# Strassen once more inside one product: S3 T3 of the second input phase as seven inner products

## The chip, the cores and the metric

The kernel runs on one core of one Trainium2 chip. The metric is the device time of that core in microseconds. TensorE multiplies; it reads both operands from the on-chip memory (SBUF) and adds into accumulators (PSUM, here eight banks of 128 x 512 float32). VectorE and ScalarE do elementwise work and can read and write PSUM. SP, ScalarE and GpSimd (POOL) issue transfers between chip memory and HBM. Every engine takes its instructions in program order and waits on semaphores.

## The reference

One layer is computed: an RMS norm, an input projection 1024 -> 2048, a causal pooling mixer, a gate, an output projection, a residual and a final norm. x has 4096 rows of 1024.

```python
normed = rms_norm(h, norm_w)
u, gate = split(normed @ in_w, 2)                       # 1024 -> 1024 + 1024
pooled = stack([trailing_mean(u_g, w) for w in (2, 4, 8, 16)]) - u   # 4 groups of 256 channels
mixed = einsum('bsgc,gcd->bsgd', pooled, group_w) + group_b
y = mixed * scale * silu(gate)
h = h + y @ out_w
out = rms_norm(h, final_norm_w)
```

Everything is float32. The kernel gets that precision from TensorE by splitting each operand into a high part (a copy rounded to the faster fp32r format) and a low part (the difference), and adding three products: high x high, high x low, low x high.

## The kernel before, in words

**Tiles.** The rows are worked in four blocks of 1024. The group map is folded into the first half of the input projection at the start, so that the kernel has two input products of 1024 x 1024 x 1024 a block (phase a and phase b, each giving 512 of u and 512 of the gate) and the output product (phase o, in eight blocks of 512 rows).

**Strassen.** Each of these products is done as seven products of half size (Winograd's form): of quarters of x and of the weights sums and differences are formed, and the seven results are added up in PSUM or on eviction. The seven are called P1 to P7; P7 is S3 T3, the product of x11 - x21 with w22 - w12. `steps` (line 960) lists them: phase a for four blocks, phase b for four blocks (order P1, P2, P6, P7, P5, P4, P3, line 32), phase o for eight. A step of phase a or b is 8 units (two halves h of the contraction by four column tiles ct), a unit is 6 matmuls of width 512 into one bank (`product_in`, 587; `mm3`, 576): 48 matmuls. A step of phase o has 24.

**Banks.** P1, P2, P7 and P4 go to banks 0 to 3, P6, P5 and P3 to banks 4 to 7 (line 585). ScalarE evicts or copies on (`evict_in`, 710), VectorE adds.

**Order of the work around a step.** The main loop (line 1204) gives, at step n: the loads for step n + 3, the sums for n + 2 (`form_in`), the split of the operands of n + 1 (`split_in`, `split_halves`: ScalarE writes the high part, VectorE the low one, into one of four operand tiles in turn, `next_op`), pooling work that is due (`pool`, about 10 us of VectorE), then the matmuls and the eviction of step n. A scheduler places the instructions of each engine by its own priorities; `tc.issue_after` holds one behind another, `tc.high_priority` moves it ahead.

**Tiles to work in.** Eleven `st` and eight `vt` tiles of 128 x 1024 are handed out by `take` and given back by `give`; a load into a tile waits until the last reader is done, and SP, which issues nearly all loads and stores, waits with it.

**Weights.** `w[i]` holds the split weights of product i, two tiles of 1 MB. Those of phase b are formed during block 3 of phase a and block 0 of phase b (`load_wb`, `form_wb`, `split_wb`), from parts in HBM: `wvd`, the folded map, and `t3d`, its difference t3, which `save_t3` (274, called at P6 of block 2, line 1249) loads, subtracts and stores. Those of phase o are formed in blocks 1 and 2 of phase b (`make_wo`, 320), stored in `wod`, and loaded and split by `load_w` (328) in block 3, each behind the step whose place it takes.

**Pooling.** `pool` (628) evaluates the trailing means, for two groups as a scan on VectorE that ScalarE starts with a short accumulated sum (`before`, 642).

Of the kernel before, what the change touches and what calls it, by code (L numbers as in the profile page):

```python
# [10 lines left out]
F32 = mybir.dt.float32  # L11
# [50 lines left out]
def kernel(  # L62
# [48 lines left out]
    ops = [mem.tile([P, 4 * H], F32R, tag=f"op{i}", name=f"op{i}") for i in range(4)]  # L111
# [42 lines left out]
    def split(dst, src):  # L154

        latest_split[1] = copy(dst[:, 0], src).ins
        latest_split[0] = sub(dst[:, 1], src, dst[:, 0].bitcast(F32)).ins
# [10 lines left out]
    wvd = [dram.tile([P, 2, H], F32, name=f"wvd{k}") for k in range(4)]  # L168
    t3d = [dram.tile([P, 2, H], F32, name=f"t3d{h}") for h in range(2)]
# [15 lines left out]
    nc.vector.memset(eps, EPS)  # L185
    scrap = const.tile([P, 1], F32, name="scrap")
# [75 lines left out]
    def load_wb(i):  # L262
        for h in range(2):
# [5 lines left out]
            for name, place, used in (("t3", t3d[h], (P6, P7)), ("22", wvd[2 + h], (P5, P3))):  # L269
                if i in used:  # L270
                    p[name] = take()
                    nc.sync.dma_start(out=p[name], in_=place)

    def save_t3():

        for h in range(2):
            us = []
            for k in (h, 2 + h):
                us.append(take())
                nc.sync.dma_start(out=us[-1], in_=wvd[k])  # L280
            with tc.issue_after(evicted[0]):
                sub(us[0], us[1], us[0])
            nc.sync.dma_start(out=t3d[h], in_=us[0])
            for u in us:
                give(u)
# [34 lines left out]
    def make_wo(h):  # L320
        us = {}
        for n in range(2):
            for kh in range(2):
                us[kh, n] = load_rows(out_w, 4 * kh + 2 * h, n * H)
                scale_rows(us[kh, n], pair(scale_c, h, kh))
        store_weights(wod, h, us[0, 0], us[1, 0], us[0, 1], us[1, 1])

    def load_w(src, i):
        for h in range(2):
            u = take()  # L330
            nc.sync.dma_start(out=u, in_=src[i][h])
            split(w[i][h], u)
# [128 lines left out]
    turn = [0]  # L461

    def next_op(pattern, **sizes):
        t = ops[turn[0] % 4]
        turn[0] += 1
        return t.rearrange(pattern, **sizes)
# [3 lines left out]
    def split_halves(us, saved=None, by_pool=False):  # L470
        ts = []
        for h, u in enumerate(us):
            t = next_op("p (s a b) -> p s a b", s=2, a=2)
# [66 lines left out]
    def split_in(q, b, i):  # L540
        s = xs[b]
        key = {P1: "11", P2: "12", P6: "2", P7: "21", P5: "11", P4: "22", P3: "12"}[i]
        later = q == 0 and b == 0 and i in (P1, P2)
# [42 lines left out]

    def product_in(i, t, sets, by_bank, between=None, behind=None):
        ps = sets[bank_of[i]]
# [3 lines left out]
        for n, (h, ct) in enumerate(halves):  # L592
            if between and n in between:
                between[n]()
            c = slice(ct * P, (ct + 1) * P)
            with tc.issue_after(behind) if behind and n == 1 else nullcontext():
                for kk in range(2):
                    mm3(
                        ps[ct],
                        (w[i][h][:, 0, kk, c], w[i][h][:, 1, kk, c]),  # L600
                        (t[h][:, 0, kk], t[h][:, 1, kk]),
                        i in (P1, P7) and h == 0 and kk == 0,
                        h == 1 and kk == 1,
                    )
        if between and 8 in between:
            between[8]()

    def product_out(i, t, sets, last):
        ps = sets[bank_of[i]]
        for j in range(2):  # L610
            rows = slice(j * P, (j + 1) * P)
            size = H // 4 if last and j == 1 else H // 2
            for c in range(0, H // 2, size):
                dst = sets["spare"] if c else ps[j]
                for k in range(4):
# [3 lines left out]
                        (t[:, 0, k, rows], t[:, 1, k, rows]),  # L619
# [8 lines left out]
    def pool(b, q, half, vs, sgs):  # L628
# [3 lines left out]
        end = HIST + H  # L632
        for g in range(2):
# [5 lines left out]
            if run_on and not first:  # L639
                for j in range(2):  # L640
                    junk = small.tile([P, HIST], F32, tag="junk", name=f"junk{b}_{half}_{grp}_{j}")
                    before = small.tile([P, 1], F32, tag="before", name=f"bf{b}_{half}_{grp}_{j}")
# [133 lines left out]
    def split_o(b, i):  # L776
        s = oxs[b]
        t = next_op("p (s a b) -> p s a b", s=2, a=4)
# [215 lines left out]
    def run(n, between=None, behind=None):  # L994
        kind, b, i = steps[n]
        sets = sets_of(kind, b)
        if kind == "o":
            product_out(i, split_up.pop(n), sets, n == len(steps) - 1)
            evict_o(b, i, sets)
        else:  # L1000
# [203 lines left out]
    for n in range(2, len(steps)):  # L1204
# [41 lines left out]
        if 0 <= since < len(ORDER_IN):  # L1246
            form_wb(ORDER_IN[since])
        run(n)
        if kind == "a" and b == 2 and i == P6:
            save_t3()  # L1250
# [71 lines left out]
```

## Time and profile before

| | us |
|---|---|
| median of 3 runs | 917.21 |
| lowest, highest | 916.2, 919.74 |
| the profiled execution's own time | 917.32 |
| its span in the profile | 915.6 |
| TensorE busy | 904.4 (99%) |
| VectorE busy | 703.5 (77%) |
| ScalarE busy | 457.5 (50%) |
| GpSimd busy | 52.6 (6%) |

In the profile's lines the engines are PE (TensorE's matmuls), PEld (its weight loads), DVE (VectorE), ACT (ScalarE), POOL (GpSimd) and SP; a q behind the name is the engine's sequencer, which issues transfers and waits. L581 is line 581. A tile is written as out<-in, without its number. A timeline line has start, length, engine, line, operation, tiles, shapes and how many in a row; in square brackets stands the idle time before it and who ended it. A line of the groups has count | busy time, mean ns of one | idle time of the engine before them. A line of the transfers ends with KB each and the median time from issue to landing. Matmuls are pipelined: one lasts 379 ns in the profile where the next starts much earlier, so the pace is read from starts.

### The profile page before, as it was taken

The page shows a single profiled execution, that of the slowest core. Times are in us where ns is not written, and L with a number is a line of the kernel's source. Part 1 is how long each engine was busy: PE and PEld are TensorE (multiplying, and loading weights), DVE is VectorE, ACT ScalarE, POOL GpSimd, SP SyncE. Part 2 cuts the span into 40 slices and gives each one's busy share as a digit, 9 for nine tenths or more (in the row PEclk, how much of TensorE's full clock was granted, in tenths as well). Part 3 has the DMA queues.
Part 4 walks back from the last instruction along what each step waited for, and adds up shares of the span by engine and source line. Part 5 has one row for each costly group of instructions (what it writes and reads, how often), then busy time and mean ns, then how long its engine had stood idle before and what let it go on. Part 6 is the DMA issues. An engine that isn't in the chain of part 4 may idle for free.

```text
span 915.6 us, 11210 instructions
## 1 busy us (share of the span) xinstructions
PE 904.4 (99%) x4212; PEld 789.0 (86%) x4212; DVE 703.5 (77%) x769; ACT 457.5 (50%) x741; POOL 52.6 (6%) x130
## 2 busy tenths in 40 slices
PE   9999999999999999999999999999999999999996
PEld 7788888888888888888888888888888888888886
DVE  3898994894699997586696589589978677676675
ACT  7869447447345565246345546654423424324333
POOL 0023201001100000000000000000101101001010
PEclk9999999999999999999999999999999999999999
DMA  9986865666756635016614725745746536356122
GB/s 340 401 320 195 316 236 166 214 230 197 264 198 241 250 146 200 24 47 238 244 47 160 257 87 194 246 161 184 252 165 227 163 135 230 128 194 216 37 92 93
DMA packets 66518, 177.02 MB, mean 193 GB/s; under 512 B 6048, under 2 KB 23840, under 8 KB 66464
## 3 DMA queue, kind: packets, MB, share of 16 engines
q1 hardware_dynamic: 59888, 154.78, 47.9%
q10 hardware_dynamic: 4176, 13.65, 3.8%
q0 software_dynamic: 2400, 7.88, 2.5%
q8 instruction: 33, 0.54, 0.2%
q14 instruction: 21, 0.17, 0.1%
HBM read 115.45 MB, written 60.83 MB: 193 GB/s over the span
## 4 chain that ended last, share of the span: by engine, by line
PE 88%; DMA 5%; DVE 3%; ACT 2%; issue 1%; SPq 0%; DVEq 0%; ACTq 0%
PE bank L581 88%; DMA early<-in_wut 2%; DMA st<-in_x 1%; DMA st<-wvd 1%; DMA st<-in_xt 1%; DVE op L146 1%; DMA t3d<-st 1%; PE bank L374 0%; DVE st L146 0%; DVE st L149 0%; ACT early L408 0%; ACT op L152 0%; DVE st L143 0%; DVE vt L143 0%; DVE vt L146 0%
## 5 line engine op out<-in xcount | busy, mean ns | idle before, releaser
L581 PE MATMUL bank<-op,w 128*128 128x512 f32 x2688 | 581.8, 379 | 2.3 <-DVE op L146 1.5
L581 PEld LDWEIGHTS bank<-op,w 128*128 128x128 f32 x2688 | 507.6, 189 | 75.7 <-DVE op L146 2.3
L581 PE MATMUL bank<-w,op 128*128 128x512 f32 (+1 forms) x1356 | 290.3, 377 | 0.0
L581 PEld LDWEIGHTS bank<-w,op 128*128 128x128 f32 x1356 | 254.6, 189 | 35.8
L146 DVE TENSOR_TENSOR op<-st,op 128x1024 fp32r<-128x1024 f32 x127 | 154.6, 1221 | 75.6 <-ACT op L152 75.5
L152 ACT ACTIVATE op<-st 128x1024 fp32r<-128x1024 f32 x127 | 133.1, 1052 | 143.8 <-PE bank L581 128.5
L152 ACT ACTIVATE vt<-bank 128x512 f32<-128x512 f32 x100 | 56.8, 593 | 49.3 <-PE bank L581 42.4
L152 ACT ACTIVATE op<-vt 128x1024 fp32r<-128x1024 f32 x39 | 40.9, 1055 | 78.8 <-PE bank L581 65.7
L924 DVE TENSOR_TENSOR st<-bank,st 128x512 f32<-128x512 f32 x60 | 41.1, 687 | 29.8 <-PE bank L581 29.4
L146 DVE TENSOR_TENSOR st<-st,st 128x1024 f32<-128x1024 f32 x35 | 42.5, 1221 | 19.3 <-DMA st<-sd 8.6
L146 DVE TENSOR_TENSOR op<-vt,op 128x1024 fp32r<-128x1024 f32 x39 | 47.5, 1222 | 9.5 <-ACT op L152 9.5
L194 POOL TENSOR_SCALAR oms<-oss 128x2 f32<-128x2 f32 x14 | 9.2, 658 | 600.0 <-ACT st L813 593.9
L152 ACT ACTIVATE bank<-bank 128x512 f32<-128x512 f32 x48 | 27.8, 580 | 30.7 <-PE bank L581 27.1
L146 DVE TENSOR_TENSOR w<-st,w 128x1024 fp32r<-128x1024 f32 x21 | 25.5, 1221 | 12.4 <-ACT w L152 12.3
L662 DVE TENSOR_TENSOR_SCAN vt<-vt,bf 128x512 f32<-128x512 f32 x28 | 34.5, 1269 | 0.2 <-ACT vt L152 0.2
L143 DVE TENSOR_TENSOR vt<-bank,vt 128x512 f32<-128x512 f32 (+1 forms) x51 | 33.2, 678 | 1.6 <-PE bank L581 1.6
L924 DVE TENSOR_TENSOR vt<-bank,vt 128x512 f32<-128x512 f32 (+1 forms) x37 | 24.8, 673 | 12.0 <-PE bank L581 11.7
L152 ACT ACTIVATE w<-st 128x1024 fp32r<-128x1024 f32 x21 | 21.9, 1053 | 17.9 <-PE bank L581 14.9
L149 DVE TENSOR_TENSOR st<-st,vt 128x1024 f32<-128x1024 f32 x23 | 27.2, 1219 | 3.1 <-DMA st<-in_xt 3.1
L684 DVE SCALAR_TENSOR_TENSOR vt<-vt,vt 128x1024 f32<-128x1024 f32 x24 | 29.1, 1214 | 0.0
L152 ACT ACTIVATE st<-bank 128x512 f32<-128x512 f32 x30 | 17.5, 595 | 22.7 <-PE bank L581 10.8
L817 DVE SCALAR_TENSOR_TENSOR st<-st,ors,st 128x1024 f32<-128x1024 f32 x17 | 21.4, 1281 | 6.1 <-POOL ors L212 6.1
(130 smaller groups left out, 556.0 us busy)
## 6 DMA issues: line engine op xcount, KB each, us to landing
st<-in_x SPq DMA_DIRECT2D x36, 512.0 KB, 5.0
st<-in_xt SPq DMA_DIRECT2D x29, 512.0 KB, 6.6
st<-sd SPq DMA_DIRECT2D x29, 512.0 KB, 5.0
sd<-st ACTq DMA_DIRECT2D x23, 512.0 KB, 3.7
vt<-in_x SPq DMA_DIRECT2D x21, 512.0 KB, 5.1
st<-yd SPq DMA_DIRECT2D x19, 512.0 KB, 4.3
yd<-vt SPq DMA_DIRECT2D x18, 512.0 KB, 2.8
out<-st SPq DMA_DIRECT2D x17, 512.0 KB, 3.6
```

What stands on the lines that cost most here:

```text
L143: nc.vector.tensor_tensor(out=dst, in0=a, in1=b, op=ALU.add)
L146: return nc.vector.tensor_tensor(out=dst, in0=a, in1=b, op=ALU.subtract)
L149: nc.vector.tensor_tensor(out=dst, in0=a, in1=b, op=ALU.mult)
L152: return nc.scalar.activation(dst, src, func)
L194: nc.gpsimd.tensor_scalar(out=ms, in0=ss, scalar1=1.0 / D, scalar2=EPS, op0=ALU.mult, op1=ALU.add)
L581: latest[0] = nc.tensor.matmul(ps, a, b, start=start and n == 0, stop=stop and n == 2, skip_group_check=True).ins
L662: nc.vector.tensor_tensor_scan(s[:, j, at:end], v[:, j, at:end], v[:, j, at - win : end - win], sums_of[j] if sums_of else 0.0, ALU.add, A ...
L684: nc.vector.scalar_tensor_tensor(out=s[:, :, at : at + H], in0=s[:, :, at : at + H], scalar=1.0 / win, in1=v[:, :, HIST:], op0=ALU.mult, o ...
L817: nc.vector.scalar_tensor_tensor(out=us[j], in0=us[j], scalar=rs[:, j : j + 1], in1=fw[0], op0=ALU.mult, op1=ALU.mult,)
L924: partial["added"] = nc.vector.tensor_tensor(out=dst, in0=src, in1=dst, op=ALU.add).ins
```

## The change

Step P7 of phase b is no longer a step of 48 matmuls of width 512. In each of the four blocks it is done as seven inner products, Winograd's form again, on quarters of S3 and T3, each of 12 matmuls of width 256.

- The operands: quarters and four sums of quarters, each split into a high and a low part of half width (`split_inner`). The operand tiles are now eight half-size ones, handed out and given back, one for the high and one for the low part.
- The results: four quarters of banks 0 to 3 (v11, v12, v21, v22). ScalarE clears v11; a quarter that enters a second result is carried on by a ScalarE copy from one PSUM quarter to the next before the following inner product adds to it: after the first, second and fourth inner product. A last difference is taken by VectorE.
- Between the inner products stand the four units of the second half of P6, the step before; P6 and P7 are evicted after that.
- The weights of the seven inner products are formed in block 1 of phase a (`form_wi`) from t3, which is now loaded, formed and saved in blocks 0 and 1, and are stored in HBM (`wid`). Four stay in the place of P7's weights during phase b. Three take the place of P3's weights and are loaded again in each block by GpSimd's queue, as P3's own weights are (`w3d`, saved in block 0).
- Loads of the output projection's weights move ahead of their use by a step (`load_wo`, `load_w` and `split_w`); the short sums for the scans share one tile of four columns a call.

```diff
-    ops = [mem.tile([P, 4 * H], F32R, tag=f"op{i}", name=f"op{i}") for i in range(4)]
+    ops = Slots([mem.tile([P, 2 * H], F32R, tag=f"op{i}", name=f"op{i}") for i in range(8)])
...
     def split_in(q, b, i):
         s = xs[b]
+        if q and i in INNER:
+            inner.update(us=s[key], sums={}, ops={})
+            with tc.high_priority():
+                split_inner(M_ORDER[:4])
+            return None
...
+    INNER = (P7,)
+    M_ORDER = (P1, P6, P2, P7, P3, P5, P4)
...
+    def split_inner(ms):
+        us, sums_in, ts = inner["us"], inner["sums"], inner["ops"]
+        q = {(h, th): quarter(us, h, th) for h in range(2) for th in range(2)}
+        for m in ms:
+            if m == P6:
+                tiles = inner["tiles"] = [
+                    take("p (m a b) -> p m a b", m=2, a=2) for _ in range(2)
+                ]
...
+                add(sums_in[P5], q[0, 1], q[1, 1])
+                sub(sums_in[P6], sums_in[P5], q[0, 0])
+            elif m == P7:
...
+                sub(sums_in[P7], q[0, 0], q[0, 1])
+            elif m == P3:
...
+                sub(sums_in[P3], q[1, 0], sums_in[P6])
...
+            ts[m] = ops.take(lambda t: t.rearrange("p (s a b) -> p s a b", s=2, a=2))
+            split((by_side(ts[m][:, 0]), by_side(ts[m][:, 1])), src)
...
+    def mm_inner(m, banks_of, j, th):
+        t, wm = inner["ops"].pop(m), wi[M_ORDER.index(m)]
+        for c in range(2):
+            ps = banks_of[2 * j + c][:, th * 256 : (th + 1) * 256].rearrange(
+                "p (a s) -> p a s", s=2
+            )
+            cols_of = slice(c * P, (c + 1) * P)
+            for kk in range(2):
+                for n, (sw, sr) in enumerate(((0, 0), (0, 1), (1, 0))):
+                    latest[0] = nc.tensor.matmul(
+                        ps, wm[:, sw, kk, cols_of],
+                        t[:, sr, kk].rearrange("p (s a) -> p a s", s=2),
+                        start=False,
...
+    def inner_product(i, sets, fill):
...
+        def carry(dst, src):
+            with tc.high_priority():
+                for c in range(2):
+                    inner["copied"] = copy(dst[c], src[c]).ins
+
+        mm_inner(P1, ps, 0, 0)
+        with tc.high_priority():
+            split_inner([P4])
+        carry(v12, v11)
+        fill.pop(0)()
+        fill.pop(0)()
+        mm_inner(P6, ps, 1, 0)
+        carry(v21, v12)
+        fill.pop(0)()
+        mm_inner(P2, ps, 0, 0)
+        mm_inner(P7, ps, 0, 1)
+        u3 = inner["tiles"][0][:, 0]
+        carry(v22, v21)
+        carry([u3[:, 0], u3[:, 1]], v21)
+        fill.pop(0)()
+        mm_inner(P3, ps, 1, 0)
+        mm_inner(P5, ps, 1, 1)
+        for c in range(2):
+            sub(u3[:, c], v22[c], u3[:, c])
+        for c in range(2):
+            add(v12[c], v12[c], u3[:, c])
+        give(inner["tiles"][0])
+        mm_inner(P4, ps, 0, 1)
...
+    def load_wi(ms):
+        for m in ms:
+            nc.gpsimd.dma_start(out=wi[m], in_=wid[m].bitcast(F32R))
...
+    def load_w3():
+        for h in range(2):
+            nc.gpsimd.dma_start(out=w[P3][h], in_=w3d[h].bitcast(F32R))
...
+    def store_wi(src):
+        behind, after = latest_split[0], evicted[0]
+        for m, b in src.items():
+            u = take("p (s a b) -> p s a b", s=2, a=2)
+            r = u.bitcast(F32R)
+            with tc.issue_after(behind):
+                with tc.issue_after(after):
+                    copy(r[:, 0], b)
+                sub(r[:, 1], b, u[:, 0])
+            nc.sync.dma_start(out=wid[M_ORDER.index(m)], in_=u)
+            give(u)
...
+        elif is_inner(n):
+            evict_in(b, 1, i, sets)
+        elif is_inner(n + 1):
+            t = split_up.pop(n)
+            clear_inner(steps[n + 1][2], sets)
+            for ct in range(4):
+                unit(i, t, sets, 0, ct)
+            give_ops(t[0])
+            with tc.high_priority():
+                split_inner(M_ORDER[4:6])
+            inner_product(
+                steps[n + 1][2], sets, [lambda ct=ct: unit(i, t, sets, 1, ct) for ct in range(4)]
+            )
...
-        if kind == "a" and b == 2 and i == P6:
-            save_t3()
...
+        if kind == "a" and b == 0 and i == P4:
+            load_t3(0)
+        elif kind == "a" and b == 0 and i == P3:
+            save_t3(0)
+            load_t3(1)
+        elif kind == "a" and b == 1 and i == P1:
+            save_t3(1)
+        if kind == "a" and b == 1:
+            k = ORDER_LATER.index(i) - 1
+            if 0 <= k < 5:
+                form_wi(k)
+        if since == 2:
+            new_wi()
+            load_wi(range(4))
...
+        if i == P3 and kind == "b" and b + 1 < NB or kind == "a" and b == NB - 1 and i == P3:
+            load_wi(range(4, 7))
+        if kind == "b" and b == 0 and i == P6:
+            load_wb(P3)
+        elif kind == "b" and b == 0 and i == P7:
+            with tc.issue_after(evicted[0]):
+                split_wb(P3)
+            save_w3()
+        elif kind == "b" and i == P7:
+            load_w3()
...
             if kind == "b" and b == NB - 1:
-                load_w(wod, i)
+                if i == P1:
+                    load_w(wod, i)
+                split_w(i)
+                if i != P3:
+                    load_w(wod, ORDER_IN[ORDER_IN.index(i) + 1])
```

194 lines of the change are left out of this document (152 added, 42 removed).

## The prediction

> **What bounds the kernel now.** I read the page's totals first, then TensorE's timeline and waits, then the other engines around the steps that the change touches.
>
> ```profile
> span 915.6 us, 11210 instructions
> PE 904.4 (99%) x4212; PEld 789.0 (86%) x4212; DVE 703.5 (77%) x769; ACT 457.5 (50%) x741; POOL 52.6 (6%) x130
> PEclk9999999999999999999999999999999999999999
> PE 88%; DMA 5%; DVE 3%; ACT 2%; issue 1%; SPq 0%; DVEq 0%; ACTq 0%
> ```
>
> TensorE is busy 99% of the span at full clock and carries 88% of the chain that ended last. Only TensorE's work, or a new wait of TensorE, can move the time. Its timeline gives the price of a product (start, us, instruction, count, idle before it):
>
> ```profile
> 0.78 3.57 PE L1026 MATMUL bank<-const-bfloat16-1.0 128*128 128x512 bf16 x8 [0.78 <-PEq L1307]
> 11.57 5.55 PE L374 MATMUL bank<-w,w 128*128 128x256 f32 x43
> ...
> 249.81 5.99 PE L581 MATMUL bank<-op,w 128*128 128x512 f32 x27
> 256.76 23.44 PE L581 MATMUL bank<-op,w 128*128 128x512 f32 x106 [0.96 <-DVE op L146]
> ...
> 861.71 10.52 PE L581 MATMUL bank<-w,op 128*128 128x512 f32 x48
> 905.74 2.84 PE L581 MATMUL bank<-w,op 128*128 128x256 f32 x24
> ```
> ```profile
> L581 PE MATMUL bank<-w,op 128*128 128x512 f32 x1332 | 287.7, 379 | 0.0
> L374 PE MATMUL bank<-w,w 128*128 128x256 f32 x48 | 6.2, 288 | 0.0
> L581 PE MATMUL bank<-w,op 128*128 128x256 f32 x24 | 2.8, 275 | 0.0
> ```
>
> The last instruction of a run overlaps nothing, so the pace is (length - one duration) / (count - 1): wide (512) (10.52 - 0.38)/47 = 215.8 ns; narrow (256) in the last products (2.84 - 0.28)/23 = 111.5 ns; narrow in the fold (5.55 - 0.29)/42 = 125 ns. One input product of 48 wide matmuls is 10.36 us. From 60 us to the end TensorE waits once:
>
> ```profile
> PE bank L581 <- DVE op L146: 1.0, 1, 1.0
> ```
>
> That is the 0.96 us at 256.76, in P1 of block 3. Unstalled, the 28th matmul after 249.81 would start at 255.64; it is 1.12 late, and the following 106 run at (23.44 - 0.38)/105 = 219.6 ns, 0.40 us above pace (a second late operand). Together 1.52 us.
>
> **The change part by part.**
>
> *Seven inner products.* Per block 48 x 215.8 = 10.36 us go and 7 x 12 = 84 narrow ones come. Bounds: 84 x 111.5 = 9.37 (-0.99) and 84 x 125 = 10.5 (+0.14). I take 111.5: those rows come from the same kind of call, with a moving operand woven from two sides like the new one; the fold reads it in one run. Four blocks: **-3.97 us** (between -3.97 and +0.6). The Trainium skill (TensorE: Matmul & The Clock Gate, Back-to-back issue gap) speaks against the change: it gives sustained pairs of weight load and matmul about 81 ns at 128 columns and 131 at 512, so by an estimate on the line between, 98 at 256, a block would lose 84 x 98 - 48 x 131 = 1.9 us and the kernel 7.8. The rows here, 215.8 and 111.5, differ from it, and they decide. The four units of P6's second half that are put in between (6 x 215.8 = 1.295 us each) are moved, not added.
>
> *t3 = v1 - v0, moved from block 2 to blocks 0 and 1.* The chain shows where the stall comes from (start, us, what):
>
> ```profile
> 222.43 5.11 DMA t3d<-st
> ...
> 227.62 5.75 DMA st<-wvd
> ...
> 234.72 0.33 SPq L283
> ...
> 235.14 7.25 DMA st<-in_xt
> ```
>
> In save_t3 the second pair of loads waits for the first store (tile reuse), the second store sits on SP until 234.72, and the x of block 3 queues behind it. After the change the loads stand a step ahead of their use, and block 2 has none of it: **-1.52 us** (0 to -1.52).
>
> *Forming the seven half weights in block 1.* VectorE gets 2 full-width and 4 + 7 half-width subtractions, ScalarE 7 half-width copies.
>
> ```profile
> 129.81:181.61 51.80, 36.63 (x39) 1.00 0.61 202
> ...
> 171.94 0.68 DVE L143 TENSOR_TENSOR st<-bank,st 128x512 f32<-128x512 f32 x1
> 172.53 1.22 DVE L146 TENSOR_TENSOR op<-st,op 128x1024 fp32r<-128x1024 f32 x1
> 176.32 1.22 DVE L146 TENSOR_TENSOR op<-st,op 128x1024 fp32r<-128x1024 f32 x1
> ```
> ```profile
> st<-in_xt SPq DMA_DIRECT2D x29, 512.0 KB, 6.6
> sd<-st POOLq DMA_DIRECT2D x6, 512.0 KB, 4.6
> t3d<-st SPq DMA_DIRECT2D x2, 512.0 KB, 4.0
> ```
>
> (The first row is a stretch, its length and VectorE's busy time.) Full width repeats every 1.14 us (the next starts before the 1.22 end), half every 0.59 (171.94 to 172.53), so 2 x 1.14 + 11 x 0.6 = 8.9 us, in five steps where VectorE is idle for 51.80 - 36.63 = 15.2: hidden as a sum. The queue is the danger: in SP's order block 2's x for P1 stands behind the stores of the half weights, in tiles that those stores free. With the weights of P3 and P5 formed by about 161 (an estimate: P6's product ends at 150.5, and ScalarE then has its eviction and some eight copies and squares of about 1 us), a store of 4.0, a load of 6.6 and one multiply give 173; behind it come the eviction of P4 and one pool step (about 5) and the two splits: some 179 and 182.7. The output phase begins at 618.2:
>
> ```profile
> L581 PE MATMUL bank<-w,op x18: 379/379/379, 618.2 to 621.9; 128*128 128x512 f32 x18
> ```
>
> Forty-two products and the 1.52 us earlier, at 181.6, P1 of block 2 starts; its splits now end at 173.75 and 177.54 (rows above). It wants the second half one bank, 1.3 us, later. The lead is used up: **+0.8 us** (0 to 2.5; nothing is taken off here, so no gain).
>
> *The carries, blocks 0 to 2.*
>
> ```profile
> L152 ACT ACTIVATE op<-st 128x1024 fp32r<-128x1024 f32 x51 | 53.4, 1050 | 41.5 <-PE bank L581 41.5
> L152 ACT ACTIVATE bank<-bank 128x512 f32<-128x512 f32 x16 | 9.3, 582 | 18.5 <-PE bank L581 18.5
> ...
> L146 DVE TENSOR_TENSOR op<-st,op 128x1024 fp32r<-128x1024 f32 x52 | 63.3, 1221 | 41.2 <-ACT op L152 41.2
> L662 DVE TENSOR_TENSOR_SCAN vt<-vt,bf 128x512 f32<-128x512 f32 x22 | 27.0, 1268 | 0.2 <-ACT vt L152 0.2
> ```
>
> A copy of 256 is estimated at 582 - 256 x (1050 - 582)/512 = 348 ns. The hand-off from TensorE is about 0.4 us: an eviction starts at 438.44, and the matmul that it waits for, the 30th of the product begun at 618.2 - 18 x 10.36 = 431.77, starts at 438.03:
>
> ```profile
> 438.44 0.60 ACT L152 ACTIVATE vt<-bank 128x512 f32<-128x512 f32 x1 [0.24 <-PE bank L581]
> ```
>
> From the start of P6's product, the first inner product ends at 6.5, two units follow, the next begins at 9.1. ScalarE by then has two high parts (their tiles come free at 5.2), a copy, the last high part, a copy: done by 8.0. The second carry has one unit: its first copy is ready at 10.5, its second at 11.2, wanted at 11.75 and 12.4. The third, four copies, by 15.5, wanted at 15.7 and 16.4. **0** in these blocks, with 0.5 to 1.2 us to spare each; the price without that cover is a rival below. VectorE gains 11 half-width and 4 quarter-width operations less two splits, about 6 us, where a block leaves it 72.5 - 57.9 = 14.7 at least (the row of block 3 below).
>
> *Block 3.* Here ScalarE's queue also carries the splits of the output weights, and the order of the changed program puts the split of P7's new weights between the first and the second carry. Its load waits for a tile that the pool's last but one operation frees. The rows: VectorE over the block, then single instructions of VectorE, SP and ScalarE.
>
> ```profile
> 545.73:618.25 72.52, 57.85 (x55) 1.00 0.58 196
> ```
> ```profile
> 551.77 1.22 DVE L146 TENSOR_TENSOR op<-st,op 128x1024 fp32r<-128x1024 f32 x1
> ...
> 560.55 3.63 DVE L662 TENSOR_TENSOR_SCAN vt<-vt,bf 128x512 f32<-128x512 f32 x3
> ...
> 567.52 1.22 DVE L684 SCALAR_TENSOR_TENSOR vt<-vt,vt 128x1024 f32<-128x1024 f32 x1
> ```
> ```profile
> 565.36 0.32 SPq L331 DMA_DIRECT2D vt<-wod  x1
> ```
> ```profile
> 568.67 1.06 ACT L152 ACTIVATE w<-vt 128x1024 fp32r<-128x1024 f32 x1 [2.62 <-DMA vt<-wod]
> ```
>
> P6 starts at 618.2 - 5 x 10.36 = 566.4. In the new order VectorE has, from the end of P2's second split (552.99) to the end of the freeing operation, 12 full-width operations (1.14), 4 scans ((3.63 - 1.27)/2 = 1.18) and 8 half-width (0.6), 23.2 in all: 576.2, or 9.8 after P6's start (now the two such pool operations stand close together and the second ends at 568.7). The load takes 3.3 (565.36 to 568.67), the weight split 1.0, the copy 0.35 and the hand-over 0.1: TensorE goes on at 14.6; it could at 5.18 + 1.34 + 2.59 + 1.34 + 1.30 + 0.3 = 12.05: **+2.5 us** (0 if the load is early, 4 if it takes 4.8). Two smaller ones: the first carry behind two weight splits and two evictions, the 0.3 just used; P6's last two banks, evicted behind four more splits, 0.5. Together **+3.3 us** (0 to 6).
>
> *Hidden.* POOL's 24 new transfers: the half weights for P3, P5, P4 have 36 us, the 2 x 1 MB of P3's weights the two products P5 and P4, 20.7 us; at 4.6 us per 512 KB one after the other they need 18.4. If the queue is slower than that, P3 waits for the difference in three blocks. Clearing, memset and the wider accumulator tile lie beside TensorE.
>
> **Sum.** -3.97 - 1.52 + 0.8 + 3.3 = -1.4 us on the profiled run's 917.32 (span 915.6 and 1.7 around it; 0.1 above the median 917.21): **915.9 us**.
>
> **Rivals.** 0.5%, 4.6 us, is about what can be told from no change: 912.6 to 921.8.
> - *Everything lands in time* (faster): only pace and the removed stall act, -5.5: 911.8. For it: the load of 565.36 shows 3.3 us, and VectorE is not saturated in block 2. Against: the order of ScalarE's queue in block 3.
> - *ScalarE misses the carries in every block* (slower). Place: three carries in each of four blocks. ScalarE is in order, and one full split (1.05) more ahead of a copy uses up the spare 0.5 to 1.2. With 1 us lost per carry beside the sum's other terms, 12 - 1.4 = +10.6: 927.9. It decides from 0.5 us per carry on (12 x 0.5 - 1.4 = 4.6). Against: ScalarE is half idle.
> - *Narrow products at 125 ns*: the count saves nothing, +0.6 - 1.5 + 0.8 + 3.3 = +3.2: 920.5. For it the fold's row, against it the 24 rows of the same call.
> - *A wait long enough for the clock*: the first eight matmuls run at (3.57 - 0.63)/7 = 420 ns, half pace. If block 3's wait reached its long end, 1.5 longer, and 16 narrow matmuls then ran at 223 instead of 111.5 (1.8), the time would be 915.9 + 3.3 = 919.2. Nothing in this trace shows a drop after a wait of 1 us. The Trainium skill (TensorE: Matmul & The Clock Gate, Part 1) says that the clock falls to half after an idle window of about 3.4 us; the trace agrees on the half pace at the start (420 against 215.8 ns) and no run here shows the window.
>
> **How the numbers follow.** Forecast 0.5 (its own range 913.5 to 919); all in time 0.17; missed carries 0.2; slow pace 0.08; clock 0.05. Faster 0.17: the first rival, most of it, and a little of the forecast's low side. Slower 0.21: missed carries and a tail of slow pace. Same 0.62. The range 911.4 to 921.5 holds all but the missed carries.
>
> **What will show it.** 336 matmuls of width 256 in phase b at a pace near 111.5 ns; no wait at P1 of block 3 in phase a; a wait of 0 to 2 us at P1 of block 2; in blocks 0 to 2 no TensorE wait on ScalarE's bank copies; in block 3 one near 2 us, with ScalarE itself waiting for a load of output weights. Wrong if phase b shows waits on copies in every block, if P3 waits for POOL's queue, or if the narrow pace is above 118 ns.

## The result, and the profile after

The changed kernel takes 923.8 us (median of 5 runs, 922.94 to 925.16) against 916.38 of the kernel before beside it: ratio 1.0077, 95% interval 1.0056 to 1.0097. It is slower by 0.8%, and the time lies above the range of 911.4 to 921.5.

The profiled execution of after took 923.75 us. First its page:

```profile
span 922.0 us, 11776 instructions
PE 902.3 (98%) x4356; PEld 790.5 (86%) x4356; DVE 728.6 (79%) x831; ACT 475.7 (52%) x806; POOL 66.1 (7%) x154
PEclk9999999999999999999999999999999999999999
PE 80%; DVE 9%; DMA 5%; ACT 4%; issue 1%; SPq 0%; DVEq 0%; ACTq 0%
```

TensorE is busy 2.1 us less (902.3 against 904.4), and the span is 6.4 us longer: waits have come in, and the chain that ended last now runs through VectorE, transfers and ScalarE for 18% (10% before). TensorE's timeline from 60 us on (start, us, instructions, count, idle before and who ended it) shows where:

```profile
133.89 208.76 PE L593 MATMUL bank<-op,w 128*128 128x512 f32 x966 [1.27 <-ACT st L152]
342.94 11.92 PE L593 MATMUL bank<-op,w 128*128 128x512 f32 x54 [0.28 <-ACT bank L152]
...
360.71 1.75 PE L677 MATMUL bank<-op,w 128*128 128x256 f32 x12 [1.90 <-ACT bank L152]
...
371.58 57.15 PE L593 MATMUL bank<-op,w 128*128 128x512 f32 x264
...
439.11 4.18 PE L677 MATMUL bank<-op,w 128*128 128x256 f32 x36
443.12 57.15 PE L593 MATMUL bank<-op,w 128*128 128x512 f32 x264
...
579.49 1.85 PE L677 MATMUL bank<-op,w 128*128 128x256 f32 x12 [3.47 <-ACT bank L152]
...
583.25 2.94 PE L677 MATMUL bank<-op,w 128*128 128x256 f32 x24 [0.61 <-ACT bank L152]
...
589.24 4.29 PE L677 MATMUL bank<-op,w 128*128 128x256 f32 x36 [1.74 <-ACT bank L152]
...
596.32 28.76 PE L593 MATMUL bank<-op,w 128*128 128x512 f32 x132 [0.21 <-ACT st L152]
```

The pace of the narrow products is (4.18 - 0.28) / 35 = 111.4 ns, and the undisturbed block from 371.58 to 443.12 takes 71.54 us where a block of before took 72.52: 0.98 us are saved in each. P1 of block 3 of phase a, where before waited at 256.76, has no row: it no longer waits. The rest are new waits, in P7 of block 1 of phase a (133.89), in block 0 of phase b (342.94 and 360.71) and in block 3 (from 579.49). Each time below is how much later than the pace TensorE goes on, with the slower first matmuls behind it:

| | forecast | profile |
|---|---|---|
| narrow products, four blocks | -3.97 | -3.9 |
| wait at P1 of block 3, phase a | -1.52 | -1.5 |
| store of t3, new wait in phase a | +0.8 | +1.5 |
| phase b, block 0 | 0 | +2.9 |
| blocks 1 and 2 | 0 | +0.3 |
| block 3 | +3.3 | +7.4 |
| sum (the profile's with -0.3 of tail and rounding) | -1.4 | +6.4 |

**Phase a and block 0.** The chain of waits of after, cut to the pieces behind the waits at 133.89 and at 360.71 (start, us, what):

```profile
125.19 7.98 DMA t3d<-st
...
133.25 0.61 ACT st L152
...
324.21 6.53 DMA yd<-st
...
330.76 4.50 DMA st<-in_in_w
...
335.29 0.07 DVE st L282
...
358.45 0.60 DVE op L146
...
360.29 0.38 ACT bank L152
...
360.71 1.31 PE bank L677 x8
```

At 133.89 an eviction of ScalarE wants the tile that the store of t3 still reads. In block 0 a store of y lands at 330.74, only then is its tile free for a load of input weights for P4, and VectorE, which is in order, stands until they have landed. Its timeline in after, and SP's in before with the same load:

```profile
335.29 1.42 DVE L282 SCALAR_TENSOR_TENSOR st<-st,colt,st 128x512 f32<-128x512 f32 x2 [7.61 <-DMA st<-in_in_w]
```
```profile
325.80 6.97 SPq L218 DMA_DIRECT2D st<-in_in_w  x2
```

The load was issued at 325.80 and is issued at 330.76 now. From 335.29 VectorE works without a gap, and the sum and low part for the second and fourth inner product come at its end.

**Block 3.** ScalarE's timeline in after; w<-vt is a split of output weights, bank<-bank of 256 a carry:

```profile
575.43 1.06 ACT L152 ACTIVATE w<-vt 128x1024 fp32r<-128x1024 f32 x1 [2.46 <-DMA vt<-wod]
578.05 0.60 ACT L152 ACTIVATE st<-bank 128x512 f32<-128x512 f32 x1 [1.56 <-DMA yd<-st]
...
579.06 0.38 ACT L152 ACTIVATE bank<-bank 128x256 f32<-128x256 f32 x1
...
581.87 1.06 ACT L152 ACTIVATE w<-vt 128x1024 fp32r<-128x1024 f32 x1 [1.51 <-DMA vt<-wod]
582.83 0.63 ACT L152 ACTIVATE bank<-bank 128x256 f32<-128x256 f32 x2
...
587.85 1.06 ACT L152 ACTIVATE w<-vt 128x1024 fp32r<-128x1024 f32 x1 [3.41 <-DMA vt<-wod]
588.82 0.37 ACT L152 ACTIVATE bank<-bank 128x256 f32<-128x256 f32 x1
```

Ahead of each carry stands a weight split that waits for its load. Ahead of the first stands also the eviction of P2's third bank, the one that the carry overwrites, and that waits for a tile which a store of y must leave first.

### The profile page after: what moved, and what is told of

Same layout as the page of the kernel before. It is cut to its first block, busy times and chain, and to the rows that moved or that the text cites. A ratio compares the mean times of both kernels' runs of the same rounds, so it can differ in the third digit from the quotient of the medians.

```text
span 922.0 us, 11776 instructions
## 1 busy us (share of the span) xinstructions
PE 902.3 (98%) x4356; PEld 790.5 (86%) x4356; DVE 728.6 (79%) x831; ACT 475.7 (52%) x806; POOL 66.1 (7%) x154
## 4 chain that ended last, share of the span: by engine, by line
PE 80%; DVE 9%; DMA 5%; ACT 4%; issue 1%; SPq 0%; DVEq 0%; ACTq 0%
PE bank L593 75%; PE bank L677 3%; PE bank L378 2%; DVE op L146 2%; DMA yd<-st 1%; DVE st L149 1%; ACT op L152 1%; DMA t3d<-st 1%; DVE vt L143 1%; DVE st L146 1%; ACT early L412 1%; DMA st<-in_x 1%; DMA early<-in_wut 1%; DVE w L146 1%; DMA vt<-wod 1%
## 5 line engine op out<-in xcount | busy, mean ns | idle before, releaser
L593 PE MATMUL bank<-op,w 128*128 128x512 f32 x2496 | 543.3, 379 | 3.6 <-ACT st L152 1.5
L152 ACT ACTIVATE op<-st 128x1024 fp32r<-128x1024 f32 (+1 forms) x139 | 137.1, 997 | 146.3 <-PE bank L593 109.1
L146 DVE TENSOR_TENSOR op<-st,op 128x1024 fp32r<-128x1024 f32 (+1 forms) x139 | 157.8, 1145 | 47.5 <-ACT op L152 40.2
L152 ACT ACTIVATE op<-vt 128x1024 fp32r<-128x1024 f32 (+1 forms) x47 | 45.4, 973 | 82.2 <-PE bank L593 61.5
L152 ACT ACTIVATE vt<-bank 128x512 f32<-128x512 f32 (+1 forms) x104 | 57.6, 595 | 51.4 <-PE bank L593 39.6
L146 DVE TENSOR_TENSOR st<-st,st 128x1024 f32<-128x1024 f32 (+2 forms) x41 | 46.9, 1153 | 20.9 <-ACT st L237 12.6
L1137 DVE TENSOR_TENSOR st<-bank,st 128x512 f32<-128x512 f32 (+1 forms) x59 | 39.8, 677 | 28.5 <-PE bank L593 28.4
L146 DVE TENSOR_TENSOR op<-vt,op 128x1024 fp32r<-128x1024 f32 (+1 forms) x47 | 52.3, 1117 | 6.4 <-ACT op L152 6.3
L677 PE MATMUL bank<-op,w 128*128 128x256 f32 x336 | 41.2, 278 | 7.7 <-ACT bank L152 7.7
L1137 DVE TENSOR_TENSOR vt<-bank,vt 128x512 f32<-128x512 f32 x38 | 26.0, 686 | 14.4 <-PE bank L593 14.1
L143 DVE TENSOR_TENSOR vt<-bank,vt 128x512 f32<-128x512 f32 x48 | 31.1, 681 | 0.6 <-PE bank L593 0.6
```

The costliest lines, as they stand in the source:

```text
L143: nc.vector.tensor_tensor(out=dst, in0=a, in1=b, op=ALU.add)
L146: return nc.vector.tensor_tensor(out=dst, in0=a, in1=b, op=ALU.subtract)
L152: return nc.scalar.activation(dst, src, func)
L593: latest[0] = nc.tensor.matmul(ps, a, b, start=start and n == 0, stop=stop and n == 2, skip_group_check=True).ins
L677: latest[0] = nc.tensor.matmul(ps, wm[:, sw, kk, cols_of], t[:, sr, kk].rearrange("p (s a) -> p a s", s=2), start=False, stop=kk == 1 and ...
L1137: partial["added"] = nc.vector.tensor_tensor(out=dst, in0=src, in1=dst, op=ALU.add).ins
```

## The experiments

The kernel before was timed again beside each group of runs. The first four runs set theory against rival for each new wait.

**t3 alone**, on the kernel before.

```diff
-        if kind == "a" and b == 2 and i == P6:
-            save_t3()
+        if kind == "a" and b == 0 and i == P4:
+            load_t3(0)
+        elif kind == "a" and b == 0 and i == P3:
+            save_t3(0)
+            load_t3(1)
+        elif kind == "a" and b == 1 and i == P1:
+            save_t3(1)
```

> The kernel before with one part of the change alone: t3 is loaded, subtracted and saved in blocks 0 and 1 of phase a, no inner products. Theory (the store of t3 itself holds back a tile that ScalarE's eviction wants while the transfer engines are full): the 1.5 us at P1 of block 3 go, and a wait of about 1.5 us comes near 132 us, in P7 of block 1; the time is that of before within 0.3 us (916.4). Rival (the eight transfers of the half weights in block 1 make that wait): no wait near 132, time 914.9. A third possibility, that moving t3 gains nothing because the wait at P1 of block 3 has another cause: 916.4 with the wait still at P1 of block 3.

916.1 us, ratio 0.9995 (0.9986 to 1.0005). From 60 us on TensorE does not wait at all: the wait at P1 of block 3 goes, and none comes near 132. The first theory missed that; no wait there is the rival's sign, but its time of 914.9 is not reached. In time, 1.5 us less is just outside the interval; what the move alone is worth is 0.5 us with about 0.9 either way. The wait at 133 was in two of the ten profiles with the whole change (after, and the run with P2's tiles taken earlier, below). In those two t3's second store lands after 8.0 and 8.8 us (in after it is also issued a microsecond later, at 125.19 against 123.4 to 124.2 in the others); in the eight others the same eviction waits for the same store too, but that lands within 6.6 to 7.6 us, in time. So the store's landing decides, and the wait is no fixed cost. What makes the landing longer stays open: with t3 alone, without the transfers of the half weights, the store lands after 7.0 to 7.1 us, and the transfer engines are fully busy from 123.4 to 131.4 (share 1.00 to 1.03) in that run as in the ten.

**The first carry ahead of the later splits.**

```diff
-            with tc.high_priority():
-                split_inner(M_ORDER[4:6])
...
         mm_inner(P1, ps, 0, 0)
-        with tc.high_priority():
-            split_inner([P4])
         carry(v12, v11)
+        with tc.high_priority():
+            with tc.issue_after(inner["copied"]):
+                split_inner(M_ORDER[4:7])
```

> The changed kernel with the first carry of each block put ahead of the splits for the inner products P3, P5 and P4 on ScalarE. Theory (in block 0 the operand of the second inner product is itself formed too late by VectorE, at 360.2, while TensorE could go on at 358.65): the wait of 2.3 us in block 0 falls only to about 1.8; block 3 is unchanged; time 923.3. Rival (ScalarE's order alone is at fault): the wait in block 0 goes to about 0.3, time 921.8.

919.61 us, ratio to before 1.0031 (1.0019 to 1.0043). Its TensorE timeline:

```profile
357.44 0.38 PE L677 MATMUL bank<-op,w 128*128 128x256 f32 x1 [0.63 <-ACT bank L152]
358.32 1.49 PE L677 MATMUL bank<-op,w 128*128 128x256 f32 x11 [0.50 <-DVE op L146]
...
576.91 2.87 PE L677 MATMUL bank<-op,w 128*128 128x256 f32 x12 [3.50 <-ACT bank L152]
```

The wait in block 0 falls to 1.6 us (1.8 was expected), and the second part of it is now for VectorE's operand itself: ScalarE's order was the smaller part. The second and third wait of block 3 are gone as well, which no theory had; the first remains. One possible reason, not tested apart, is the clock: behind the first wait TensorE runs at half pace (granted clock 0.57 over 4 us, 1.7 us lost), which gives ScalarE that much time for the next carries; the next run, with block 3 unchanged, has the same (0.58) and only 0.5 us idle at the later carries. The time is below the forecast of 923.3: those two waits are missing, and this profile also has no wait at 133.

**P4's weight split later**, behind P7 of block 0.

```diff
-        if 0 <= since < len(ORDER_IN) and ORDER_IN[since] not in (P7, P3):
+        if 0 <= since < len(ORDER_IN) and ORDER_IN[since] not in (P7, P3, P4):
             with tc.issue_after(evicted[0]):
                 split_wb(ORDER_IN[since])
...
                 split_wb(P3)
+                split_wb(P4)
```

> The changed kernel with the split of P4's phase-b weights (two full-width operations of VectorE and two of ScalarE) moved from P1 of block 0 behind P7 of block 0. Theory (VectorE is full in block 0 and these operations stand ahead of the inner sums): 2 x 1.14 us less ahead of the sum for the second inner product, so the 2.3 us at it go to 0 to 0.3, and the 0.55 us at P2 of block 0 may go too; time 921.2. Rival (the pooling work, not the weights, makes the inner sums late): the wait stays above 1.5 us, time 923 or more.

922.26 us, ratio 1.0062 (1.0047 to 1.0077). The wait at the second inner product of block 0 is as in the changed kernel; only the small one at P2 goes:

```profile
359.10 2.32 PE L677 MATMUL bank<-op,w 128*128 128x256 f32 x12 [1.91 <-ACT bank L152]
```

The theory falls. The 2.3 us of VectorE were taken off, and other work, the full-width sums for P5 and P3, moved into their place ahead of the inner operands.

**The output weight splits behind the last carry**, block 3.

```diff
-                split_w(i)
+                with tc.issue_after(inner["copied"]) if i in (P6, P7) else nullcontext():
+                    split_w(i)
```

> The changed kernel with the splits of the output weights of P6 and P7 in block 3 held on ScalarE and VectorE behind the last carry; tiles and transfers are the same. Theory with two causes: the waits of 0.9 us and 2.0 us ahead of the second and the third carry go; the first one of 4.0 us stays above 2.5, since the eviction of P2's bank, which the carry overwrites, waits for a tile that a store of y frees at about 578; together about 3.5 us, time 920.3. Rival (the splits' waits for their loads are the only cause): all 7 us of block 3 go, time 916.8.

921.69 us, ratio 1.0061 (1.0041 to 1.008). TensorE waits once in block 3, and ScalarE ahead of it for the tile alone (one row of TensorE's timeline, one of ScalarE's):

```profile
578.20 2.93 PE L677 MATMUL bank<-op,w 128*128 128x256 f32 x12 [3.16 <-ACT bank L152]
```
```profile
576.79 1.08 ACT L152 ACTIVATE st<-bank 128x512 f32<-128x512 f32 x2 [5.09 <-DMA yd<-st]
```

With the splits away the second and the third wait go, the first stays at 3.3 us, as the theory of two causes had it. Behind it 1.6 us more were lost to a lower clock (last section), so that this run alone does not tell what the splits did from what the slower pace did; the next one has no fall of the clock in block 3.

**P2's tiles taken earlier as well.**

```diff
-            ev["11"] = [take() for _ in range(2)]
+            ev["11"] = ev.pop("early", None) or [take() for _ in range(2)]
...
                 if i == P1:
+                    ev["early"] = [take() for _ in range(2)]
                     load_w(wod, i)
```

> As in the run before it, the splits of P6's and P7's output weights are held behind the last carry; besides, the two tiles into which P2 of block 3 is evicted are taken a step earlier, so that they are not tiles which a store of y must free first. Theory with two causes (late loads, and that tile): no wait of TensorE is left in block 3 but up to 0.5 us at its end; block 0 keeps its 2 us wait (and, if the granted clock falls after it, up to 1.9 us more). Time 917 to 918. Rival (a third cause, such as the inner operands formed too late by VectorE in block 3 as well): a wait of over 1 us stays in block 3.

916.45 us, ratio 1.0001 (0.9989 to 1.0013), 7 us less than the changed kernel and a little below the 917 to 918 expected. Block 3 has no wait left; its second and third inner products follow without idle time:

```profile
576.01 1.50 PE L677 MATMUL bank<-op,w 128*128 128x256 f32 x12
577.35 1.46 PE L593 MATMUL bank<-op,w 128*128 128x512 f32 x6
578.65 2.84 PE L677 MATMUL bank<-op,w 128*128 128x256 f32 x24
```

That settles block 3. This profile still has the waits of block 0 (1.11 and 1.90 us idle) and the one at 133.

**The sums for P5 and P3 behind the inner splits**, on the changed kernel.

```diff
-        if i == P6 and (q or b):
+        if i == P6 and b and not q:
             form_s4(b)
...
+        behind_inner = kind == "b" and i == P6
-        if n > 2 and not normal:
+        if n > 2 and not normal and not behind_inner:
             form(n + 2)
         advance("split", n, split_step, split_reach)
+        if behind_inner:
+            with tc.issue_after(latest_split[0]):
+                form_s4(b)
+                form(n + 2)
```

> The changed kernel with the four full-width sums for P5 and P3 of phase b held on VectorE behind the splits of the first four inner products. Theory (in block 0 they and the pooling work stand in VectorE's order ahead of the low part of the second inner product, which ends at 357.4 to 359 instead of some 355): the 2 us wait of block 0 falls below 0.8, block 3 keeps its 5 to 7 us; time 920 to 922. Rival (pooling alone makes it late): the wait stays above 1.5.

925.1 us, ratio 1.01 (1.0085 to 1.0114). The wait in block 0 falls to 1.0 us, a little above the 0.8 expected. But tiles are handed out in another order, and block 3 has a new wait at P2, since ScalarE stands at the split of the first output weights (TensorE's row, then ScalarE's):

```profile
561.09 13.61 PE L593 MATMUL bank<-op,w 128*128 128x512 f32 x54 [4.05 <-ACT bank L152]
```
```profile
558.55 1.06 ACT L152 ACTIVATE w<-st 128x1024 fp32r<-128x1024 f32 x1 [7.30 <-DMA st<-wod]
```

Half pace follows this wait and one of 2.5 us at the second carry (granted clock 0.59 and 0.57 over 4 us), and the time misses the 920 to 922 expected.

**All five edits** above on the changed kernel; their diffs are those shown.

> All five edits together: first carry ahead of the later inner splits, sums for P5 and P3 behind the inner splits, P4's weight split later, output weight splits behind the last carry, P2's tiles of block 3 taken earlier. If these waits are all that the inner products lose, phase b takes 290.1 - 4.0 = 286.1 us and the time is that of the kernel with t3 moved alone less 4.0: 912.1, faster than before by 0.5%. Rival (work that is held back makes new waits later, in P5, P4 or P3 or at the start of the output phase): 914 to 917.

918.78 us, ratio 1.0025 (1.0013 to 1.0037): the rival. Block 0 is mended but for 0.6 us at P2. In block 3, whose first inner product now starts 4.4 us sooner than with P2's tiles alone taken earlier (567.7 against 572.1), pooling scans stand ahead of the inner sums on VectorE; ScalarE stands 5.7 us for a sum, TensorE behind it, and half pace follows (granted clock 0.60 over 4 us):

```profile
574.39 0.38 PE L677 MATMUL bank<-op,w 128*128 128x256 f32 x1 [2.59 <-ACT bank L152]
575.80 2.03 PE L677 MATMUL bank<-op,w 128*128 128x256 f32 x11 [1.03 <-DVE op L146]
```
```profile
571.10 0.63 ACT L152 ACTIVATE op<-vt 128x512 fp32r<-128x512 f32 x1 [5.74 <-DVE vt L146]
```

The row of 335.29 above shows VectorE's stand at the late load. Three runs move work out of its way.

**P4's weights formed behind P2's split**, with both edits of block 3.

```diff
-            form_wb(ORDER_IN[since])
+            with tc.issue_after(latest_split[0]) if ORDER_IN[since] == P4 else nullcontext():
+                form_wb(ORDER_IN[since])
```

> Both edits for block 3 (output weight splits behind the last carry, P2's tiles taken earlier) and, for block 0, the forming of P4's weights held on VectorE behind the split of P2's operand; every tile and transfer stays where it was. Theory (in block 0 VectorE stands idle for 7 us at 328 to 335, since a load of input weights for P4 comes late, and all that follows, the inner sums too, is late by that): with 3.4 us of its work done in that time the second inner product's operand is ready by 355, so the 2 us wait at it goes and the 0.5 to 1.3 us at P2 of block 0 too; phase b has no wait over 0.6 us. Time 912 to 913.5. Rival (VectorE is simply too full in block 0): a wait of over 1 us stays at the second inner product, time 915 or more.

912.98 us, ratio 0.9962 (0.9949 to 0.9974). No wait at the inner products is left; 1.2 us came at the start of P6 in block 0, above the 0.6 that was allowed for, and 0.5 in the output phase.

**The same edit alone** on the changed kernel, run last.

> The changed kernel with one edit: the forming of P4's weights in block 0 is held on VectorE behind the split of P2's operand; block 3 is left as it is. Theory (VectorE's stand at the late load makes all of block 0's loss): the waits at P2 and at the second inner product of block 0 go (2.9 us in the profile), up to 1.2 us come at the start of P6 as in the run with block 3 mended too; block 3 keeps some 7 us; time 921.5 to 923. Rival (block 0 went well in the run with all waits mended only because block 3's edits moved tiles): the wait at the second inner product stays above 1.5 us, time 923.5 or more.

920.63 us, ratio 1.004 (1.0024 to 1.0057), 0.9 better than the range. The waits at P2 and at the second inner product go, but in the profile more than expected comes at P6, where the forming and splitting of P4's weights now stands ahead of P6's operand.

```profile
351.86 6.64 PE L593 MATMUL bank<-op,w 128*128 128x512 f32 x23 [4.19 <-DVE op L146]
```

TensorE is 4.4 us late here, and 1.5 us more go at half pace; in the kernel before this one it is 1.2 us late. The two kernels differ in block 3 alone, and from 300 us up to this wait VectorE, ScalarE and SP have the same instructions in the same order. But the profiled execution here is the longest of seven, 924.71 us against the median of 920.63. In it a load of t3 comes later (VectorE waits 5.1 us for it, 3.5 in the other), the stores of y behind it are issued 1.75 us later, and ScalarE's next evictions wait for a tile that such a store holds, which they do not in the other profile:

```profile
330.05 1.08 ACT L152 ACTIVATE vt<-bank 128x512 f32<-128x512 f32 x2 [5.28 <-DMA yd<-vt]
```

So the edit of VectorE's order alone moves some 1.2 us of the lateness on to P6; the other 3.2 us, as far as two profiles can tell, belong to this execution and not to the edit. In block 3 the first wait, 4.1 us, is followed by 3.0 us at half pace, and the second and the third do not come.

**P4's weights formed behind the inner splits and split behind the last carry**, with both edits of block 3.

```diff
-        if 0 <= since < len(ORDER_IN) and ORDER_IN[since] not in (P7, P3):
+        if 0 <= since < len(ORDER_IN) and ORDER_IN[since] not in (P7, P3, P4):
             form_wb(ORDER_IN[since])
+        elif since == 7:
+            with tc.issue_after(latest_split[0]):
+                form_wb(P4)
...
+        elif since == 7:
+            with tc.issue_after(inner["copied"]):
+                split_wb(P4)
```

> As the kernel beside it, but P4's weights are formed only behind the splits of the first four inner operands and split behind the last carry of block 0, so that VectorE never stands at their load; the tiles that they hold are given back later, and tiles are handed out in another order. Theory: no wait at the inner products of block 0, time 912 to 913.5. Rival (tiles held longer bring new waits elsewhere, as the run with all five edits had): a wait of over 1 us in another place, time 914 to 917.

911.53 us, ratio to before 0.9951 (0.9938 to 0.9965): faster than both kernels, by 0.5% and 1.3%. TensorE does not wait once between 60 us and the end. Its page and the inner products of block 0 in its timeline:

```profile
span 909.5 us, 11772 instructions
```
```profile
352.12 1.50 PE L677 MATMUL bank<-op,w 128*128 128x256 f32 x12
353.46 2.76 PE L593 MATMUL bank<-op,w 128*128 128x512 f32 x12
356.05 1.50 PE L677 MATMUL bank<-op,w 128*128 128x256 f32 x12
```

This is the first rival's time (911.8): the inner products are worth about what the count says once nothing is late. Against the kernel before beside it the gain is 4.5 us, 3.2 to 5.7 by the interval; the rival's 5.5 lies in it, and so do the 3.97 of the narrow products alone.

The two runs that made waits on purpose belong to the clock and stand in the last section.

## Why the prediction was wrong

The forecast was -1.4 us and a time of 915.9; the profile has +6.4. The step that failed is the waits at the carries: 0 in block 0 and 3.3 us in block 3 were forecast, 2.9 and 7.4 measured, 7.0 of the 7.8 us between forecast and profile. What the runs show in their place: loads that come late (in block 0 because a store of y still holds the tile) and an eviction that waits for a tile under a store, standing ahead of the carries and of their operands on in-order engines.

- *Pace.* Right: 111.4 ns, -0.98 us a block. The Trainium skill (TensorE: Matmul & The Clock Gate, Back-to-back issue gap) spoke for a loss of 7.8 us; the rows disagree with it, 111.4 ns against an estimate of 98 and 215.8 against 131.
- *The wait at P1 of block 3 in phase a.* Right as a wait: it is in none of the runs with t3 moved. In time the move alone is worth 0.5 us, with about 0.9 either way, not clearly the 1.52.
- *+0.8 at P1 of block 2.* Wrong in place and cause. Block 2's x was in time. What was late is a tile under the store of t3, in P7 of block 1, and that only in two profiles of ten.
- *The carries in blocks 0 to 2: 0.* Right in blocks 1 and 2. In block 0 this step failed, by 2.9 us. It followed ScalarE instruction by instruction from the start of P6, and took the operands as formed; for VectorE it counted only a sum over a block (14.7 us left). The block has that time, but 7.6 us of it are spent standing at a load before the inner sums, and the load is late because its tile is freed by a store. A sum over a stretch says nothing on an in-order queue that is late within it.
- *Block 3: +3.3.* The mechanism was right (ScalarE's splits of output weights, waiting for loads, ahead of the carries); the sizes were off, 7.4 in place of 3.3. Of the terms, the first carry measured 4.0 for 0.3, the second 0.9 for 2.5, the third 2.0 for 0, P6's last banks 0.5 for 0.5. For the first, the load of P6's weights was not followed, only that of P7's, and the dependency on P2's eviction was missed: in the kernel before that tile had until P7, 10.36 us on; the first carry overwrites the bank and wants it 6.5 us after P6's start.
- *Hidden transfers.* Right: no P3 in phase b waits for POOL's queue.
- *The rivals.* Missed carries came true in two blocks of four, and not by ScalarE's own load but by what it waits for. All in time is the time that the mended kernel reaches. The clock is below: its price of 1.8 us lies among those measured (1.4 to 3.2), but the wait that it asks for, 4 us, was too long.

## What to carry to other kernels

Where a change asks for a result earlier than before, follow every instruction that stands ahead of it on its in-order engine back to the load or the tile that it waits for; a total of idle time on that engine does not tell it. With tiles handed out in turn, look for loads and evictions that get the tile of a store just issued: here two such tiles cost about 6 us. An edit that takes or gives a tile at another point reassigns the tiles of everything behind it, and an edit of order alone can push the lateness on, so each has to be looked at in later blocks too.

## What the runs showed of the hardware

After waits of TensorE the matmuls ran at half pace for 2.9 to 6.3 us, in kernels where the page's row of 40 slices, or the mean clock of the run, hardly shows it. Two runs on the kernel before made waits on purpose, with copies of a bank over one that the next product starts anew; the first only at P1 and only over the first bank, the second over all four banks.

```diff
+        if i in waits:
+            k = waits[i][counts[i]]
+            counts[i] += 1
+            if k:
+                with tc.high_priority():
+                    for _ in range(k):
+                        copy(ps[0], sets["y"][3])
+                    for c in range(1, 4):
+                        copy(ps[c], ps[0])
```

> The kernel before, with a wait made at the start of P1 in seven blocks: ScalarE copies a bank 2, 4, 6, 1, 3, 8 and 12 times over one that P1 then starts anew, some 0.52 us each behind the last matmul of the step before (results unchanged). It prices the clock: in the runs so far waits of about 2 to 3.6 us were followed in four of eight places by 2 to 4 us at half pace (granted clock 0.66 to 0.77 of the stretch). Theory (a fall comes where TensorE idled most of a fixed stretch of time, so from about 2 us on by chance and always for 4 us and more): full pace after waits of about 0.9 to 1.5 us, half pace for some after 2 to 3 us, and always after 4.5 and 6.5 us. Rival (it depends on what runs, not on the wait): no half pace at all in these wide products.

926.85 us, one run. The lengths did not come out as planned, and only four of the seven show as waits of TensorE on ScalarE; why is not shown. Idle times of 0.65 to 1.43 us were followed by full pace, one of 3.11 by a granted clock of 0.57 over 4 us.

> The kernel before, with waits made at P1 of seven blocks and at P7 of the four blocks of phase b: ScalarE overwrites the first bank k times and the other three from it before the product starts them anew (results unchanged), k being 3, 2, 5, 3, 4, 2, 6 and 3, 4, 2, 8; waits of about 0.4 + 0.52 k, so 1.4 to 4.6 us. Theory (the clock falls after a wait of about 2 us or more, by chance below 2.5): full pace after waits under 1.7 us, half pace of 1.3 to 1.9 us in cost after those over 2.6 us, some of each between. Rival (a wait must be over 3.4 us): half pace only after the waits of over 3.4 us.

979.01 us, one run; waits of 0.25 to 10.89 us, longer than planned. Its timeline at three waits, and the 4 us behind each (length, engines' busy times, then the granted clock, the share and rate of the transfers):

```profile
193.34 75.61 PE L581 MATMUL bank<-op,w 128*128 128x512 f32 x336 [3.25 <-ACT bank L152]
...
480.23 38.12 PE L581 MATMUL bank<-op,w 128*128 128x512 f32 x174 [1.89 <-ACT bank L152]
522.39 36.79 PE L581 MATMUL bank<-op,w 128*128 128x512 f32 x161 [4.04 <-ACT bank L152]
```
```profile
193.30:197.30 4.00, 3.96 (x9) 2.95 (x10) 4.00 (x5) 1.45 (x5) 0.00 (x0) 0.50 0.47 188
...
480.20:484.20 4.00, 3.98 (x17) 3.09 (x18) 1.88 (x2) 1.56 (x3) 0.00 (x0) 1.00 0.81 310
522.40:526.40 4.00, 4.00 (x11) 3.27 (x12) 3.12 (x3) 0.92 (x2) 0.00 (x0) 0.60 0.32 131
```

Over all profiles: no fall after idle times up to 1.74 us; after five of 1.89 to 1.91 us, two falls; after seventeen of 2.5 us and more, sixteen falls (one, after 2.59 us, only behind a second wait of 1.03 us close by). The one without is the wait of 3.47 us in after. By the granted clock in windows of half a microsecond, ten of the eighteen falls last 3.4 us and cost 1.7 us on top of the wait; the other eight, all at half pace from TensorE's first matmul on, last 2.9 to 6.3 us and cost 1.4 to 3.2. Two windows of the same length, 4 us behind the same wait of 1.9 us in block 0, in the runs with P4's split later and with P2's tiles taken earlier:

```profile
359.10:363.10 4.00, 4.00 (x17) 3.56 (x18) 1.36 (x3) 2.46 (x5) 0.00 (x0) 0.63 0.56 199
```
```profile
360.90:364.90 4.00, 3.95 (x28) 3.72 (x29) 3.68 (x5) 2.51 (x5) 0.00 (x0) 1.00 0.27 87
```

So a wait of TensorE of about 2 us can cost nearly twice its length, in two cases of five here, and one of 2.5 us or more nearly always brings 1.4 to 3.2 us on top. The rival with a threshold of 3.4 us falls. The Trainium skill (TensorE: Matmul & The Clock Gate, Part 1) has an activity window of about 3.4 us that runs free of the kernel; the ten falls of 3.4 us agree with it, and that equal waits end differently fits a window that runs free, while a fall after 1.9 us of idle time shows that the window need not be idle from end to end.
